# A decoder step with paged attention on one core: a second tile for the sample's new rows, key and query loads placed by rules of their own, row sums in the ring of probability tiles

## The chip, the cores and the metric

The kernel runs on 1 core of one Trainium2 chip. The metric is the time of one execution in microseconds (us) as the device measures it; three runs of the kernel before gave 3022.00, 3025.98 and 3029.27 us, median 3025.98 us. A profile is one further execution with its trace.

## The reference

One inference step of a two-layer decoder in float32: a recurrent layer (RG-LRU), then an attention layer with forgetting. It runs for a prompt (one sequence of 2048 new tokens) and for a sample (8 sequences of 8 new tokens, each behind 4096 cached tokens that lie in 32 pages of 128 rows, found through a page table). 16 heads of 64.

```python
def fox_block(q, k, v, cq, ck, q_pos, k_pos):
    s = jnp.einsum('bqhd,bkhd->bhqk', q, k).astype(jnp.float32) * (HEAD_DIM ** -0.5)
    s = s + jnp.swapaxes(cq, 1, 2)[:, :, :, None] - jnp.swapaxes(ck, 1, 2)[:, :, None, :]
    mask = k_pos[None, :] <= q_pos[:, None]
    s = jnp.where(mask[None, None], s, -jnp.inf)
    p = jax.nn.softmax(s, axis=-1)
    return jnp.einsum('bhqk,bkhd->bqhd', p.astype(v.dtype), v)
...
        past_k = cache_k[page_table].reshape(Bs, past_len, N_HEADS, HEAD_DIM)
        past_v = cache_v[page_table].reshape(Bs, past_len, N_HEADS, HEAD_DIM)
...
        y = fox_mixer(rms_norm(x, b_pre_norm[l]), k_all, v_all, cq, ck, q_pos, k_pos, b_w_in[l], b_w_out[l])
        x = x + rms_norm(y, b_post_norm[l])
```

The kernel returns the outputs of both groups, the new keys, values and log-forget rows, and the recurrent states.

## The kernel before, in words

The stages follow each other on one core: the recurrent layer in two chunks, the projections to keys, values, queries and gates, attention, the output projection. The change lies in two pieces of code that run beside each other.

**`attention` (from line 1332)** does the prompt. Work goes by units: a unit `u` is a head `h` and a quarter `qc` of 512 query rows, 64 units in all; odd heads take the quarters in the opposite order. Inside a unit each tick handles one tile of 128 keys against the 512 queries: two matmuls into a score bank `st` (lines 1592 and 1593), an exponential on ScalarE (line 1601) into a probability tile `p` (tag `p`, 6 buffers) or, for the first tick of a unit, into `acc`; after four ticks, and two more of delay, the product with the values (`ops`, line 1612), and additions of `p` to `acc` on GpSimd (POOL). A head has 40 ticks.

The exponential needs each query row's maximum first. `top` (line 1421) works it out some 18 to 26 ticks ahead of the unit: matmuls `sx` of the queries `qbt` with the keys `kbt` (line 1431), and a maximum on VectorE (lines 1433 and 1435). The `sx` banks are 3. `tops` then writes the maxima into four more rows of `qbt` (`mps`, lines 1448 and 1450). So `qbt` is needed by `top` first and by the unit's score matmuls later; it has 6 buffers (`NQ`), `kbt` has 2, one for even and one for odd heads. `load_unit` (line 1413) and `load_keys` (lines 1399 and 1400) fill them. Before the change `advance` loads the next unit's `qbt` when the first `top` of a unit is due, and the keys of the next head are loaded behind the first tick of a head. Other loads (`load_low`, `load_head`, the gates at line 1521) are emitted inside `with paged()`.

When a head's four units are through, `total` sums their `acc` over partitions (`tot`, line 1481), ScalarE copies the result to `cs` (line 1484), a tile of its own, and a DMA spreads it into `sums` (line 1490); `norm` makes reciprocals (line 1495), sends them through a DMA (line 1501) and a matmul `rp` (line 1505), and stores the gated output (line 1511).

**`decode` (from line 1039)** does the sample: 16 turns, one for each sequence and half of the heads; turns from the fourth on run beside the projections and attention (`ahead` is true there). A turn brings 32 pages of keys and 32 of values in groups of four by DMAs on the SP queue (`pages`, line 1093, 256 KB each, tile `raw`, 4 buffers of a group each), transposes the keys on VectorE (`ktr`, line 1180), multiplies (`dS`, line 1148), makes a softmax, and multiplies with the pages of values (`dO`, line 1262). The 8 new rows of keys and of values of the sample come by `new_rows` (line 1103) into `rawn`, one zeroed tile for both: the keys' rows are read by a transpose at the turn's fifth page group (line 1158), the values' rows by a product at the turn's end (line 1270).

Order: all loads of attention and decode but the very first are issued on the SP queue, one after the other; a DMA whose buffer is in use holds all behind it. A scheduler fixes the order of every queue when the program is built: it takes instructions by priority (the order in which the code emits them) and by its own estimate of when each is ready, so that one may overtake another that would have to wait. Buffers with one tag are handed out in the order in which the tiles are asked for. `paged()` adds an edge: what is issued inside stands behind the newest page that has been emitted.

Of the kernel before, what the change touches and what calls it, by code (L numbers as in the profile page):

```python
# [11 lines left out]
F32 = mybir.dt.float32  # L12
# [8 lines left out]
P = 128  # L21
# [6 lines left out]
H = 16  # L28
# [20 lines left out]
LEAD = 18  # L49
# [7 lines left out]
NP = 6  # L57
ADD = "G"
OG = 1
NQ = 6  # L60
# [21 lines left out]
def f(ap):  # L82

    return ap.bitcast(F32)
# [3 lines left out]
def tile_hawk_fox(  # L88
# [8 lines left out]
    V, A, G, T, S = nc.vector, nc.scalar, nc.gpsimd, nc.tensor, nc.sync  # L97
# [19 lines left out]
    def paged():  # L117

        return tc.issue_after(place["S"]) if "S" in place else ExitStack()
# [49 lines left out]
    def dt_(name, shape):  # L169
        return dram.tile(shape, F32, name=name, tag=name)  # L170
# [13 lines left out]
    ks_d, vs_d = dt_("ksd", [NSAMP, D]), dt_("vsd", [NSAMP, D])  # L184
# [37 lines left out]
    def sbuf(es, name, side=None):  # L222
        return es.enter_context(tc.tile_pool(name=name, bufs=1, side=side, reuse_waits="tile"))
# [819 lines left out]
    def decode(es, turns, nraw, nktr, ahead):  # L1043
        pool = sbuf(es, "dec", "right")
# [4 lines left out]
        qmask = pool.tile([P, DS], F32, name="qmask")  # L1049
        V.tensor_reduce(qmask[:, :], ident[:, :].rearrange("p (a q) -> p q a", q=DS), axis=AX.X, op=ALU.add)  # L1050

        rawn = pool.tile([P, 512], F32, name="rawn")
        G.memset(rawn[:, :], 0.0)
        pcs = [pool.tile([P, 64], F32, name=f"dpc{i}") for i in range(2)]
        for pc in pcs:
            G.memset(pc[:, :], 0.0)
# [43 lines left out]
        def new_rows(rows, b, hg):  # L1100

            assert known >= {("k" if rows is ks_d else "v", hg * 2 + c) for c in range(2)}
            S.dma_start(rawn[:DS, :], rows[b * DS:(b + 1) * DS, hg * 512:(hg + 1) * 512])
            return rawn

# [228 lines left out]
    def attention(es):  # L1334
        pool = sbuf(es, "att")
# [4 lines left out]
        pool.tile([P, 512], F32, name="acc", tag="acc", bufs=NACC)  # L1340
        pool.tile([P, 512], F32, name="p", tag="p", bufs=NP)
        pool.tile([P, 512], F32, name="oT", tag="oT", bufs=5)
        pool.tile([P, 512], F32, name="cs", tag="cs")
        pool.tile([P, 512], F32, name="sgt", tag="sgt", bufs=2)
        vvs = [pool.tile([P, 16, HD], F32, name=f"vvt{i}") for i in range(2)]
        pool.tile([P, SEQ], F32R, name="ka", tag="ka", bufs=2)
# [36 lines left out]
        units = [(h, qc) for h in range(H) for qc in ((0, 1, 2, 3) if h % 2 == 0 else (3, 2, 1, 0))]  # L1383
# [5 lines left out]
        def halves(h):  # L1389
            return ((0, half), (half, SEQ)) if h == 0 else ((0, SEQ),)  # L1390
# [4 lines left out]
        def load_keys(h):  # L1395
            kb = kbs[h % 2]
            loaded.add(h)
            for lo, hi in halves(h):
                queue[0].dma_start(f(kb[0:64, lo:hi]), kd_d[h * HD:(h + 1) * HD, 1, lo:hi])
                queue[0].dma_start(f(kb[64:67, lo:hi]), nc_d[h, :, lo:hi])  # L1400
# [9 lines left out]
        def load_unit(u):  # L1410
            h, qc = units[u]
            assert u < done[2] + NQ
            queue[0].dma_start(f(qbs[u % NQ][0:64, :]), qd_d[h * HD:(h + 1) * HD, 0, qc * 512:(qc + 1) * 512])

        def load_low(u):
            if u < len(units):
                h, qc = units[u]
                qa = qas[u] = pool.tile([P, 512], F32R, name="qa", tag="qa", bufs=4)
                queue[0].dma_start(f(qa[:, :]), qd_d[h * HD:(h + 1) * HD, :, qc * 512:(qc + 1) * 512].rearrange("d x t -> (d x) t"))
# [56 lines left out]
        def total(h2, sums, todo, single):  # L1476


            ps = ps3.tile([P, 512], F32, name="tot", tag="sx", bufs=3)
            for qc, acc in todo:  # L1480
                T.matmul(ps[qc * 32:(qc + 1) * 32, :], ones[:, :32], acc[:, :], start=True, stop=True)
            cs = pool.tile([P, 512], F32, name="cs", tag="cs")
            rows = slice(0, P) if len(todo) == 4 else slice(qc * 32, (qc + 1) * 32)
            A.copy(cs[rows, :], ps[rows, :])
            if single:
                for qc, acc in todo:
                    j = qc * 2 + h2
                    S.dma_start(sums[j * 16:(j + 1) * 16, :], cs[qc * 32:qc * 32 + 1, :].rearrange("o (r c) -> o r c", r=16))
            else:
                S.dma_start(sums[h2 * HD:(h2 + 1) * HD, :], cs[:, :].rearrange("(q z) (r c) -> z q r c", z=32, r=16)[0])  # L1490
# [37 lines left out]
        nks = [(qc + 1) * 4 for _, qc in units]  # L1528
        start = [sum(nks[:u]) for u in range(len(units))]
        done = [0, 0, 0]  # L1530

        def advance(tick):

            need = 0
            for u in range(len(units)):
                need = max(need, start[u] + nks[u] - 2 * max(0, start[u] - min(LEAD, RAMP + tick) - tick))
                if start[u] > tick + 40:
                    break
            while done[0] < min(need, len(tasks)):
                u, j, ck = tasks[done[0]]  # L1540
                while done[1] <= min(u + 1, len(units) - 1):
                    load_unit(done[1])
                    done[1] += 1
                top(u, j, ck)
                done[0] += 1

        load_keys(0)
        tick = 0
# [12 lines left out]
        def scores_bank():  # L1561

            if dec_done:
                wide[0] += 1
                if wide[0] % 2:
                    return psum["dec"].tile([P, 512], F32, name="st", tag="do"[wide[0] // 2 % 2], bufs=1)
            return ps3.tile([P, 512], F32, name="st", tag="st", bufs=2)
# [3 lines left out]
        def loads():  # L1571
            while lows[0] < len(units):
                v = lows[0]
                if tick < (start[v - 2] if v < 4 else min(max(start[v - 2], start[v - 3] + AFT), start[v] - 3)):
                    break
                with paged():
                    load_low(v)
                lows[0] += 1
            h, k = divmod(tick, 40)
            if k == 16 and h + 1 < H:  # L1580
                with paged():
                    load_head(h + 1)

        for u, (h, qc) in enumerate(units):
            for k in range(nks[u]):
                loads()
                ka, kb = heads[h], kbs[h % 2]
                qa, qb = qas[u], qbs[u % NQ]
                lo = max(0, k - qc * 4) * P
                ks = slice(k * P, (k + 1) * P)  # L1590
                ps = scores_bank()
                place["T"] = T.matmul(ps[:, lo:], ka[:, ks], qa[:, lo:], start=True, stop=False).ins  # L1592
                T.matmul(ps[:, lo:], kb[:, ks], qb[:, lo:], start=False, stop=(k < qc * 4))  # L1593
                if k >= qc * 4:
                    T.matmul(ps[:, lo:lo + P], identB[:, :], causal[:, :], start=False, stop=True)
                done[2] = u + (k == nks[u] - 1)
                if k == 0:
                    p = acc = pool.tile([P, 512], F32, name="acc", tag="acc", bufs=NACC)
                else:
                    p = pool.tile([P, 512], F32, name="p", tag="p", bufs=NP)  # L1600
                pair.append((k, lo, p, A.activation(p[:, lo:], ps[:, lo:], AF.Exp)))  # L1601

                def product(u=u, h=h, todo=pair, acc=acc, last=(k == nks[u] - 1)):


                    nonlocal ops
                    if todo[0][0] == 0:
                        ops = ops2[:, u % 2 * 256:u % 2 * 256 + 256]

                    def mm(k, lo, p, r):  # L1610
                        a0 = (lo // P + 1 - r) // 2
                        return T.matmul(ops[r * HD:(r + 1) * HD, a0 * P:], vvs[h % 2][:, k, :],  # L1612
                                        p[:, :].rearrange("p (a r c) -> p a r c", a=2, r=2)[:, a0:, r, :],
                                        start=(k == 0), stop=(last and k == todo[-1][0] - 1 + r))

                    together([partial(mm, k, lo, p, r) for k, lo, p, _ in todo for r in range(2) if lo <= (2 + r) * P],
                             [todo[-1][3]])
                    for k, lo, p, _ in todo:
                        if k:
                            tt(a_l(), acc[:, lo:], acc[:, lo:], p[:, lo:], ALU.add)  # L1620
                    if last:
                        finish(u, ops, acc)

                if k % 4 == 3:
                    later.after(2, product)
                    pair = []
                before = done[0]
                advance(tick)
                tick += 1
                later.tick()  # L1630
                if k + sum(nks[u - u % 4:u]) == 0 and h + 1 < H:
                    load_keys(h + 1)
                yield 4.1 * (512 - lo) * 0.42 + (done[0] - before) * 213

    lent, dec_done = {}, []
# [1 line left out]
    rows = [(NSAMP, None, x1s_d[:, :], ys_flat)]  # L1637
# [151 lines left out]
    done = 9  # L1789
# [6 lines left out]
    done = max(done, 41)  # L1796
# [104 lines left out]
```

## Time and profile before

| | us |
|---|---|
| median of 3 runs | 3025.98 |
| profiled execution, its own time | 3028.43 |
| span of that execution's trace | 3026.4 |
| TensorE busy (PE) | 2803.4 |
| VectorE busy (DVE) | 1805.5 |
| ScalarE busy (ACT) | 1269.9 |
| GpSimd busy (POOL) | 1084.4 |

The span is the trace from its first to its last instruction; the execution's own time is 2.0 us longer. PE is TensorE's matmuls, PEld its weight loads, SPq the SP queue as it issues DMAs. An arrow in a row (`out<-in`) names what is written and read, `x16` counts instructions, and the bracket behind a row of the timeline gives the idle time of the engine before it with what ended it. A row of waits gives who waited, for whom, the total, the number and the longest. The granted clock is TensorE's, as a share of full speed.

### The profile page before, as it was taken

How to read it: one execution, taken by the hardware profiler on the slowest of the kernel's cores; microseconds unless marked ns; L12 is line 12 of the kernel's file. 1: busy time of each engine (PE TensorE's matmuls, PEld its weight loads, DVE VectorE, ACT ScalarE, POOL GpSimd, SP SyncE). 2: the span in 40 equal slices, each digit the busy share in tenths (PEclk: the TensorE clock that was granted, in tenths of full speed). 3: DMA queues.
4: the chain of work that ended last, by engine and by line, in shares of the span. 5: the costliest groups of instructions: out<-in, count | busy, mean ns of one | idle time of the engine just before them, and what ended most of it. 6: DMA issues, size and time to landing. Idle time of an engine off the chain costs nothing.

```text
span 3026.4 us, 60467 instructions
## 1 busy us (share of the span) xinstructions
PE 2803.4 (93%) x21614; PEld 2252.1 (74%) x21614; DVE 1805.5 (60%) x4012; ACT 1269.9 (42%) x2874; POOL 1084.4 (36%) x1199
## 2 busy tenths in 40 slices
PE   6998999998997999999999699998998999999998
PEld 5997789988887997888889556665665666565687
DVE  6877455425427775676564466656776756655344
ACT  4665342222125665534333234444544444355321
POOL 1653201000002653100000245665575656659422
PEclk9999999999998999999999889999999999999999
DMA  4224546888863226699999968898899888874343
GB/s 123 79 88 133 171 126 191 256 263 281 278 216 91 89 88 194 209 313 338 332 346 326 279 209 243 248 282 255 250 291 287 267 251 265 260 247 122 98 145 110
DMA packets 479103, 653.79 MB, mean 216 GB/s; under 512 B 91291, under 2 KB 277020, under 8 KB 471525
## 3 DMA queue, kind: packets, MB, share of 16 engines
q1 hardware_dynamic: 475174, 644.26, 67.4%
q10 hardware_dynamic: 3340, 3.56, 0.4%
q8 instruction: 171, 2.80, 0.4%
q0 software_dynamic: 288, 2.10, 0.2%
q14 instruction: 130, 1.06, 0.1%
HBM read 514.22 MB, written 135.16 MB: 215 GB/s over the span
## 4 chain that ended last, share of the span: by engine, by line
PE 59%; DMA 16%; DVE 9%; ACT 6%; SPq 5%; issue 3%; POOL 1%; ACTq 0%; DVEq 0%; POOLq 0%
PE ops L1612 7%; PE st L1592 4%; PE y L383 4%; PE y L384 4%; PE y L385 4%; DMA raw<-in_cache_k_dram 4%; PE sx L1431 4%; PE dO L1262 3%; DMA raw<-in_cache_v_dram 3%; PE st L1593 3%; PE dS L1148 3%; PE kv L383 3%; PE kv L385 3%; PE kv L384 3%; SPq L1093 2%
## 5 line engine op out<-in xcount | busy, mean ns | idle before, releaser
L108 POOL TENSOR_TENSOR acc<-acc,p 128x512 f32<-128x512 f32 (+3 forms) x576 | 640.9, 1114 | 347.7 <-PE ops L1612 211.2
L1601 ACT ACTIVATE p<-st 128x512 f32<-128x512 f32 (+3 forms) x576 | 291.3, 525 | 400.1 <-PE st L1593 177.5
L1180 DVE STREAM_TRANSPOSE ktr<-raw 128x1024 f32<-128x1024 f32 x256 | 308.2, 1226 | 125.1 <-DMA raw<-in_cache_k_dram 116.5
L1433 DVE TENSOR_REDUCE mxs<-sx 128x1 f32<-128x512 f32 x384 | 255.0, 681 | 141.0 <-PE sx L1431 139.6
L383 PE MATMUL kv<-wh,xh 128*128 128x256 f32 (+3 forms) x1088 | 310.0, 288 | 6.4 <-ACT wh L427 4.7
L384 PE MATMUL kv<-wl,xh 128*128 128x256 f32 (+3 forms) x1088 | 309.3, 287 | 5.7 <-DVE wl L428 5.7
L385 PE MATMUL kv<-wh,xl 128*128 128x256 f32 (+3 forms) x1088 | 309.6, 286 | 2.7 <-DMA xl<-xld 2.7
L1592 PE MATMUL st<-qa,ka 128*128 128x512 f32 (+3 forms) x640 | 269.9, 422 | 13.3 <-ACT p L1601 7.5
L1612 PE MATMUL ops<-p,vvt 128*64 128x256 f32 (+1 forms) x2176 | 262.9, 369 | 1.0 <-ACT p L1601 0.7
L1431 PE MATMUL sx<-kbt,qbt 96*128 96x512 f32 (+3 forms) x640 | 229.2, 416 | 29.9 <-DMA qbt<-qd 24.2
L1113 POOL TENSOR_TENSOR qw<-qb,amask 128x128 f32<-128x128 f32 x64 | 29.1, 460 | 618.1 <-PE dS L1148 325.3
L428 DVE SCALAR_TENSOR_TENSOR wl<-wst,gv,wh 128x256 fp32r<-128x256 f32 (+1 forms) x384 | 169.4, 504 | 131.8 <-ACT wh L427 131.5
L427 ACT ACTIVATE wh<-wst,gv 128x256 fp32r<-128x256 f32 (+1 forms) x384 | 164.6, 499 | 190.2 <-DMA wst<-in_w_kv_dram 72.7
L1593 PE MATMUL st<-qbt,kbt 128*128 128x512 f32 (+3 forms) x640 | 236.9, 370 | 0.0
L383 PE MATMUL qg<-xh,wh 128*128 128x512 f32 (+2 forms) x640 | 229.4, 359 | 0.0
L384 PE MATMUL qg<-xl,wh 128*128 128x512 f32 (+2 forms) x640 | 228.2, 357 | 0.0
L385 PE MATMUL qg<-xh,wl 128*128 128x512 f32 (+2 forms) x640 | 227.5, 356 | 0.6 <-DVE wl L428 0.6
L1612 PEld LDWEIGHTS ops<-p,vvt 128*64 128x64 f32 x2176 | 161.5, 141 | 88.2 <-issue 19.8
L383 PEld LDWEIGHTS kv<-wh,xh 128*128 128x128 f32 (+1 forms) x1088 | 203.5, 188 | 13.2 <-ACT wh L427 6.8
L384 PEld LDWEIGHTS kv<-wl,xh 128*128 128x128 f32 (+1 forms) x1088 | 203.2, 188 | 10.1 <-DVE wl L428 6.9
L385 PEld LDWEIGHTS kv<-wh,xl 128*128 128x128 f32 (+1 forms) x1088 | 204.8, 188 | 7.0 <-issue 3.7
L1592 PEld LDWEIGHTS st<-qa,ka 128*128 128x128 f32 x640 | 123.7, 193 | 112.8 <-issue 54.4
(297 smaller groups left out, 6356.3 us busy)
## 6 DMA issues: line engine op xcount, KB each, us to landing
raw<-in_cache_k_dram SPq DMA_DIRECT2D x512, 256.0 KB
raw<-in_cache_v_dram SPq DMA_DIRECT2D x512, 256.0 KB
wst<-in_w_kv_dram SPq DMA_DIRECT2D x48, 512.0 KB
wst<-in_b_w_in_dram SPq DMA_DIRECT2D x48, 512.0 KB
xt<-in_x_prompt_dram SPq DMA_DIRECT2D x32, 512.0 KB
wst<-in_a_w_in_dram SPq DMA_DIRECT2D x64, 256.0 KB
out_dram<-kf SPq DMA_DIRECT2D x128, 128.0 KB
sc<-cd SPq DMA_DIRECT2D x16, 1024.0 KB
```

The source lines that it names most:

```text
L108: eng.tensor_tensor(out, a, b, op=op)
L383: T.matmul(ps, lh(k), rh(k), start=(k == 0), stop=False)
L384: T.matmul(ps, lh(k), rl(k), start=False, stop=False)
L385: T.matmul(ps, ll(k), rh(k), start=False, stop=(k == nk - 1))
L428: V.scalar_tensor_tensor(wl[:, k, :], st[:, k, :], gk, f(wh[:, k, :]), op0=ALU.mult, op1=ALU.subtract)
L1180: behind("V", V.transpose(t.kts[pp][:, n], raw[:, :, pp * 256:(pp + 1) * 256]).ins)
L1431: T.matmul(ps[:, :w], qb[0:96, j * P:(j + 1) * P], kb[0:96, ck * 512:ck * 512 + w], start=True, stop=True)
L1433: place["V"] = V.reduce_max(mx[:, j, ck:ck + 1], ps[:, :w], axis=AX.X).ins
L1592: place["T"] = T.matmul(ps[:, lo:], ka[:, ks], qa[:, lo:], start=True, stop=False).ins
L1593: T.matmul(ps[:, lo:], kb[:, ks], qb[:, lo:], start=False, stop=(k < qc * 4))
L1601: pair.append((k, lo, p, A.activation(p[:, lo:], ps[:, lo:], AF.Exp)))
L1612: return T.matmul(ops[r * HD:(r + 1) * HD, a0 * P:], vvs[h % 2][:, k, :], p[:, :].rearrange("p (a r c) -> p a r c", a=2, r=2)[:, a0:, r, : ...
```

## The change

Four edits:

- In the second `decode` (`ahead`) `rawn` becomes two tiles; the keys' rows go to the last, the values' rows to the first.
- The tile `cs` loses its own buffer and is taken from tag `p`, the ring of six probability tiles.
- `advance` now loads a unit's queries only where they are still missing; the regular place is in `loads`, at the head of a tick: as soon as the unit's start is no more than `LEAD` + half its ticks + 7 ticks away and a buffer is handed back, inside `paged()`.
- The next head's keys are loaded in `loads` at tick 6 of a head, inside `paged()`, and no longer behind its first tick.

```diff
-        rawn = pool.tile([P, 512], F32, name="rawn")
-        G.memset(rawn[:, :], 0.0)
+        rawns = [pool.tile([P, 512], F32, name=f"rawn{i}") for i in range(2 if ahead else 1)]
+        for rawn in rawns:
+            G.memset(rawn[:, :], 0.0)
...
+            rawn = rawns[-1 if rows is ks_d else 0]
             S.dma_start(rawn[:DS, :], rows[b * DS:(b + 1) * DS, hg * 512:(hg + 1) * 512])
...
-        pool.tile([P, 512], F32, name="cs", tag="cs")
...
-            cs = pool.tile([P, 512], F32, name="cs", tag="cs")
+            cs = pool.tile([P, 512], F32, name="cs", tag="p", bufs=NP)
...
-                while done[1] <= min(u + 1, len(units) - 1):
+                while done[1] <= u:
                     load_unit(done[1])
...
+            while done[1] < len(units) and done[1] < done[2] + NQ and tick >= start[done[1]] - LEAD - nks[done[1]] // 2 - 7:
+                with paged():
+                    load_unit(done[1])
+                done[1] += 1
             h, k = divmod(tick, 40)
+            if k == 6 and h + 1 < H:
+                with paged():
+                    load_keys(h + 1)
...
-                if k + sum(nks[u - u % 4:u]) == 0 and h + 1 < H:
-                    load_keys(h + 1)
```

The lines of the changed kernel lie one to eight higher than those of the kernel before. Three places show what the change does to the order.

The SP queue early in attention, between a group of key pages and the next group of value pages (`raw`). Before, with the two query tiles, and the values' rows in the one `rawn`:

```order
L1413 DMA qbt0_19863<-qd_78 64x512
L1103 DMA rawn_14345<-vsd_83 8x512
L1413 DMA qbt1_19864<-qd_78 64x512
L1086 TENSOR_LOAD pt1_115
L1093 ISA
L1093 DMA raw_20436<-in_cache_v_dram 128x512
```

Now:

```order
L1105 DMA rawn0_14345<-vsd_83 8x512
L1105 DMA rawn1_14346<-ksd_82 8x512
L1087 TENSOR_LOAD pt1_115
L1094 ISA
L1094 DMA raw_20437<-in_cache_v_dram 128x512
```

Both row DMAs stand there one behind the other (before, the keys' rows stood two pages further ahead, among the key pages), and the two query loads have moved behind later pages.

ScalarE's queue at the end of the third head, with the copy `cs` and the exponentials around it. Before (the exponentials into `p_22848` and its followers run ahead of the copy):

```order
L1601 ACTIVATE p_22766<-st_22763 128x512
L1601 ACTIVATE p_22843<-st_22840 128x512
L1601 ACTIVATE p_22848<-st_22845 128x512
L1601 ACTIVATE p_22865<-st_22862 128x512
L1601 ACTIVATE p_22870<-st_22867 128x512
L1601 ACTIVATE p_22891<-st_22888 128x512
L1601 ACTIVATE p_22904<-st_22901 128x512
L1601 ACTIVATE p_23002<-st_22999 128x512
L1601 ACTIVATE p_23014<-st_23011 128x512
L1601 ACTIVATE p_23026<-st_23023 128x512
L1601 ACTIVATE p_23052<-st_23048 128x512
L1450 ACTIVATE qbt1_19864<-mps_22728,less_19908 4x128 x4
```

and behind these stands the copy `cs_22773`. Now (`p_22842` here is what `p_22843` was):

```order
L1609 ACTIVATE p_22760<-st_22757 128x512
L1609 ACTIVATE p_22765<-st_22762 128x512
L1451 ACTIVATE qbt1_19865<-mps_22729,less_19909 4x128 x4
L1485 COPY cs_22772<-tot_22767 128x512
L1609 ACTIVATE p_22842<-st_22839 128x512
L1609 ACTIVATE p_22847<-st_22844 128x512
L1609 ACTIVATE p_22864<-st_22861 128x512
L1609 ACTIVATE p_22871<-st_22868 128x512
```

The copy has moved ahead of ten exponentials. The last row is the one that takes the copy's buffer again, so it waits for the DMA that reads `cs`.

TensorE's queue at the end of the first head, around the sums `tot`. Before:

```order
L1448 MATMUL mps<-ident,mrow_19901 128x128
L1481 MATMUL tot<-acc,ones 32x512 x4
L1431 MATMUL sx<-kbt_19870,qbt_19863 128x512
L1612 MATMUL ops<-p,vvt_19860 64x256 x8
L1592 MATMUL st<-qa,ka 128x512
L1593 MATMUL st<-qbt_19867,kbt_19870 128x512
```

Now:

```order
L1449 MATMUL mps<-ident,mrow_19902 128x128
L1482 MATMUL tot<-acc,ones 32x512 x4
L1432 MATMUL sx<-kbt_19871,qbt_19864 128x512
L1432 MATMUL sx<-kbt_19871,qbt_19864 128x128
L1432 MATMUL sx<-kbt_19871,qbt_19864 128x512
L1432 MATMUL sx<-kbt_19871,qbt_19864 128x256
L1432 MATMUL sx<-kbt_19871,qbt_19864 128x512
L1432 MATMUL sx<-kbt_19871,qbt_19864 128x384
L1432 MATMUL sx<-kbt_19871,qbt_19864 128x512
L1620 MATMUL ops<-acc,vvt_19861 64x256 x2
L1620 MATMUL ops<-p,vvt_19861 64x256 x6
L1600 MATMUL st<-qa,ka 128x512
```

Seven row-maximum products stand between `tot` and the next score product, where one stood; the `sx` of the unit after have been pulled forward.

## The prediction

> **What bounds the kernel now.** I read the page's busy times first, then the windows of the stage that the change touches, then who waits for whom there, then the order in time around the waits. Columns of a window: engine busy us and instructions, then the granted TensorE clock, DMA share and GB/s.
>
> ```profile
> PE 2803.4 (93%) x21614; PEld 2252.1 (74%) x21614; DVE 1805.5 (60%) x4012; ACT 1269.9 (42%) x2874; POOL 1084.4 (36%) x1199
> 1800.00:2700.00 900.00, 846.08 (x7720) 540.37 (x7720) 587.35 (x1252) 409.88 (x1017) 561.91 (x535) 0.97 0.85 264
> PE dO L1262 <- DMA raw<-in_cache_v_dram: 19.1, 12, 3.1
> PE st L1592 <- ACT p L1601: 5.6, 16, 0.8
> ```
>
> TensorE is the bound: 2803 of 3026 us over the whole program, and 846 of 900 us in the stage where attention runs beside the sample's decode. There it stands still for 54 us. The largest single cause is 19.1 us in 12 waits of the value products (dO) for pages of cached values. Such a page is late when the SP queue, which issues all pages, stood behind something else:
>
> ```profile
> SPq L1093 <- PE dO L1262: 33.0, 12, 7.3
> SPq L1413 <- PE st L1595: 20.7, 9, 5.3
> SPq L1399 <- PE sx L1431: 16.5, 2, 16.0
> SPq L1413 <- PE sx L1431: 13.7, 13, 6.1
> SPq L1103 <- DVE mrow L1444: 9.0, 1, 9.0
> ```
>
> Between 1740 and 2740 us the queue stood behind query loads (L1413), key loads (L1399) and the sample's new rows (L1103) for some 60 us (the last four rows), and behind page buffers that a product had not yet freed (the first row) for 33. The change touches the three former and not the latter. A wait of SP costs nothing by itself; it costs where a product then stands still.
>
> **The change part by part.** First, the tile of new rows. Early in attention the queue had this order (start, duration, line, operation):
>
> ```profile
> 1760.57 0.45 SPq L1413 DMA_DIRECT2D qbt<-qd  x1
> 1770.05 0.30 SPq L1103 DMA_DIRECT2D rawn<-vsd  x1
> 1771.67 0.45 SPq L1413 DMA_DIRECT2D qbt<-qd  x1
> 1780.41 2.34 SPq L1093 DMA_DIRECT2D raw<-in_cache_v_dram  x4
> 1800.79 1.07 PE L1262 MATMUL dO<-raw,sx 128*32 128x256 f32 x16 [2.18 <-DMA raw<-in_cache_v_dram]
> 1798.00:1808.00 10.00, 7.82 (x47) 4.83 (x46) 5.92 (x11) 2.88 (x5) 1.36 (x2) 0.83 1.03 346
> ```
>
> Three small DMAs took 20 us of the queue: the values' rows had to wait until the keys' rows had been read from the one tile, and both query tiles until their last readers were through. In the changed order both row DMAs stand directly ahead of those value pages, each with a tile of its own, and the two query loads stand behind later pages. I take back the 2.18 us wait, and the clock that followed it: 0.83 granted over 10 us is 1.7 us of lost work. Together **3.9 us**. The same pattern with a query load alone:
>
> ```profile
> 1910.90 6.26 SPq L1413 DMA_DIRECT2D qbt<-qd  x1
> 1917.76 1.94 SPq L1093 DMA_DIRECT2D raw<-in_cache_v_dram  x4
> 1924.24 1.20 PE L1262 MATMUL dO<-raw,sx 128*32 128x256 f32 x16 [2.08 <-DMA raw<-in_cache_v_dram]
> 1924.00:1932.00 8.00, 7.76 (x140) 5.71 (x144) 2.13 (x6) 2.79 (x7) 5.03 (x7) 0.79 1.02 319
> ```
>
> The load held the queue for 6.26 us, the pages went out behind it, and TensorE waited 2.08 us; 0.79 over 8 us is 1.7 us more. I take all of it, **3.8 us**. Two other places I take in part:
>
> ```profile
> 1980.10 1.09 SPq L1413 DMA_DIRECT2D qbt<-qd  x1
> 1988.37 1.94 PE L1262 MATMUL dO<-raw,sx 128*32 128x256 f32 x16 [3.10 <-DMA raw<-in_cache_v_dram]
> 1986.00:1996.00 10.00, 7.63 (x94) 5.27 (x94) 2.90 (x7) 1.13 (x3) 1.74 (x2) 0.66 0.83 258
> 2097.71 1.07 PE L1262 MATMUL dO<-raw,sx 128*32 128x256 f32 x16 [0.91 <-DMA raw<-in_cache_v_dram]
> 2106.64 1.07 PE L1262 MATMUL dO<-raw,sx 128*32 128x256 f32 x16 [1.86 <-DMA raw<-in_cache_v_dram]
> 2117.49 1.07 PE L1262 MATMUL dO<-raw,sx 128*32 128x256 f32 x16 [0.76 <-DMA raw<-in_cache_v_dram]
> 2126.07 1.07 PE L1262 MATMUL dO<-raw,sx 128*32 128x256 f32 x16 [1.15 <-DMA raw<-in_cache_v_dram]
> 2090.00:2130.00 40.00, 35.11 (x390) 22.12 (x388) 22.45 (x40) 13.42 (x29) 29.12 (x25) 1.00 0.85 273
> ```
>
> At 1988 the query load held the queue for only 1.09 us: I take 1.1 of the 3.1 us, and half of the clock (0.66 over 10 us is 3.4), **2.8 us**. The four waits around 2110 sum to 4.7 us at full clock; a row DMA, a key load and a query load lie among their pages, and I take half, **2.3 us**. The other dO waits, 19.1 − 12.0 = 7.1 us, I leave. Gain: 3.9 + 3.8 + 2.8 + 2.3 = **12.8 us**.
>
> What is late next is what the change adds. The copy of the row sums (cs) now takes a place in the ring of six probability tiles, and holds it until its DMA has landed:
>
> ```profile
> 1909.52 0.58 ACT L1484 COPY cs<-tot 128x512 f32<-128x512 f32 x1
> 1920.28 0.69 SPq L1490 DMA_DIRECT2D sums<-cs  x1
> 1925.18 0.35 DVE L1495 RECIPROCAL sums<-sums 128x32 f32<-128x32 f32 x1 [2.60 <-DMA sums<-cs]
> 2187.69 0.58 ACT L1484 COPY cs<-tot 128x512 f32<-128x512 f32 x1
> 2188.30 0.62 SPq L1490 DMA_DIRECT2D sums<-cs  x1
> ```
>
> From copy to issue it took between 0.0 us (2188) and 10.2 us (1920), and another 4.2 us to land (1920.97 to 1925.18). In the changed order the place is wanted again by the fourth score tile behind the copy at six of the first thirteen head ends, later at the others. Queued behind the waiting exponential on ScalarE are the next ones, and TensorE stands once its two score banks are full. Those two banks and the row-maximum products beside them are the cover; without it this costs up to 5 us a head, 0 to 30 us at the six. I take 1.8 us, by the rows nearest to it: the exponentials' present waits for their ring cost TensorE 5.6 us in 16 places.
>
> Further, the exponentials behind a copy may no longer pass it, and the order fills the gap with row-maximum products (sx): over the whole order, places with six or more of them between two score products go from 2 to 12.
>
> ```profile
> L1433 DVE TENSOR_REDUCE mxs<-sx 128x1 f32<-128x512 f32 x313 | 208.1, 681 | 118.0 <-PE sx L1431 116.9
> L1431 PE MATMUL sx<-kbt,qbt 96*128 96x512 f32 (+3 forms) x527 | 185.5, 409 | 5.3 <-DVE mxs L1435 2.6 <-DVE mxs L1433 1.3 <-ACT qbt L1450 0.8
> ```
>
> VectorE takes 0.68 us each, TensorE 0.41, with three banks between: six in a row cost at most 3 × 0.27 = 0.8 us, ten places 0 to 8 us. I take 1.2, since all present waits of that kind are 2.6 + 1.3 us. Queries and keys loaded later I cost at nothing (0 to 17 us, see the rivals); the cover is SP's lead over TensorE, which the 33.0 us row shows, since there SP waits for TensorE. ScalarE issues one query load less at the start of attention; that is at most one issue (0.45 us above), taken at nothing. The second clearing of a tile is one POOL instruction on an engine 36% busy. Cost: **3.0 us**.
>
> Sum against the profiled execution's own time: 3028.4 − 12.8 + 3.0 = 3018.6. That execution was 2.4 us above the median of the runs, so I give **3016 us** beside 3026.
>
> Of the 12.8 us, 5.1 are clock. The Trainium skill, page "TensorE: Matmul & The Clock Gate", section "Part 1: The HAM clock gate (the "warmup" mystery)", says that the rate halves after about one idle window of 3.4 us. By that rule none of these waits would cost clock, and the result would be 3021. The trace does not agree: behind waits of 2.18 and 2.08 us the windows show 0.83 and 0.79; behind four shorter ones 1.00. I go by the windows.
>
> **The rivals.** *The page buffers take over (no change).* A query load that no longer blocks only lets the queue reach the next page, whose buffer may be in use: the 33.0 us row. And this row pair shows 16 us of blocked queue behind a key load, after which the only wait of TensorE in the next 37 us was the third row:
>
> ```profile
> 2637.12 0.39 SPq L1419 DMA_DIRECT2D qa<-qd  x1
> 2653.51 0.46 SPq L1399 DMA_DIRECT2D kbt<-kd  x1
> PE st L1592 <- ACT p L1601: 0.6, 1, 0.6
> ```
>
> Also the key loads hardly move in the order: 0 to 6 pages later. If gain and cost are both about 3 us: **3026**. Chance 0.14. With the clock kept as the page's rule has it (3021), 0.04 more.
>
> *The sums hold the ring (slower).* There are as many score tiles as sx products, 527 in 900 us, one per 1.7 us; the fourth tile wants the place 6.9 us after the copy. A DMA out 9 us after it, as it nearly was at 1920, has landed at 9 + 0.7 + 4.2 = 13.9, so the exponentials stop for 7.0 us; two banks cover 3.4, leaving 3.6 us and 1.7 us of clock. At four of the six heads that is 21 us: 3028.4 − 12.8 + 1.2 + 21 − 2.4 = **3035**. It decides once the DMA leaves more than some 5 us after the copy. For it: the order puts the copies 3 to 10 score tiles earlier, their DMAs only 0 to 8 pages. Against: at 2188 the queue was there at once. Chance 0.20.
>
> *Queries come too late (slower).* The load for unit 15 stood behind page 536 of the 1024 and now stands behind page 568, its first use behind the 131st score tile; unit 56's load went from page 980 to 1004, its use is behind the 535th. At the present pace these are:
>
> ```profile
> 1975.31 0.50 PE L1592 MATMUL st<-qa,ka 128*128 128x512 f32 x1 [0.28 <-ACT p L1601]
> 2675.77 0.33 SPq L1093 DMA_DIRECT2D raw<-in_cache_v_dram  x1
> 2678.01 0.23 PE L1592 MATMUL st<-qa,ka 128*128 128x128 f32 x1
> ```
>
> Page 568 is out at 1980.1, 4.8 us after the first; page 1004 only 2.2 us ahead of the last. With 4.5 us to land (1919.7 to 1924.2) that is 9.3 and 2.3 us, with 3.4 and 1.7 us of clock 16.7 us, so 3028.4 − 9.8 + 16.7 − 2.4 = **3033**. It decides once SP is less than 4.5 us ahead. Chance 0.17.
>
> **How the numbers follow.** Forecast 0.45, no change 0.18, ring 0.20, queries 0.17. Low end: the remaining 7.1 us of dO waits and their clock (3.4) go too and the costs are nil, 3016 − 13.5 = 3002. High end: the slower rivals with some of each other, 3044. Faster by over 0.2% 0.45, within 0.2% (6 us, about what a measurement of this kernel can tell from no change) 0.18, slower 0.37.
>
> **What would show it.** Right: the queue's waits under the query loads and row DMAs fall from 43 us (three rows above) to under 20, dO waits for value pages to about 9 us, and the windows around 1800 and 1924 show a full clock. Ring: TensorE waits for exponentials rise well above 5.6 us, and SP's sums follow the copies by 8 us. Queries: a wait of sx for a query DMA appears inside the stage, where none is now. Wrong altogether: dO still waits some 19 us.

## The result, and the profile after

| | before | after |
|---|---|---|
| median us (lowest to highest) | 3024.66 (3022.00 to 3029.27) | 3102.89 (3095.99 to 3111.29) |
| profiled execution: own time, span, clock | 3028.43, 3026.4, 0.969 | 3095.99, 3094.3, 0.960 |

The ratio is 1.0258, 95% interval 1.0225 to 1.0291: slower by 78 us, where 3016 was forecast and the range ended at 3044. The loss lies between the first and the last of the 640 score products (`st`). There TensorE's trace reads:

| first to last score product | length | TensorE busy | idle | longer than before, behind head ends | elsewhere |
|---|---|---|---|---|---|
| before | 1074.8 | 1011.7 | 63.0 | | |
| after | 1146.1 | 1040.4 | 105.7 | 84.3 | -12.9 |

"Behind head ends" are the first 20 score products of each of the heads 1 to 15, nearly half of the work. All of the loss is there. The 84.3 us hold some work that the order has moved there from elsewhere (4096 matmuls of TensorE where there were 3966), which is why the rest is shorter than before; net it is 71 us, 4.8 us a head. In the whole stretch 43 us of the loss are idle time, and 29 us are the same work (8863 and 8866 matmuls) at a lower clock.

Views of the kernel after, first the windows of the same stretches as before (busy us and instructions of PE, PEld, DVE, ACT, POOL, then the granted clock, DMA share, GB/s):

```profile
1800.00:2700.00 900.00, 819.60 (x7384) 522.47 (x7386) 566.49 (x1192) 386.13 (x954) 531.02 (x509) 0.95 0.81 249
1798.00:1808.00 10.00, 9.44 (x56) 5.48 (x56) 7.30 (x14) 4.62 (x11) 2.18 (x2) 0.97 0.77 271
1924.00:1932.00 8.00, 8.00 (x122) 4.58 (x120) 2.52 (x8) 4.13 (x10) 5.28 (x7) 1.00 0.85 267
```

The two places where I had counted the gain run at 0.97 and 1.00 of the clock, and yet TensorE does 336 matmuls fewer in the 900 us. Who waits for whom there, TensorE first:

```profile
PE mps L1449 <- DVE mrow L1445: 21.0, 8, 7.6
PE st L1600 <- ACT p L1609: 12.2, 20, 2.6
PE sx L1432 <- DVE mxs L1436: 11.8, 8, 4.5
...
PE dO L1264 <- DMA raw<-in_cache_v_dram: 5.8, 2, 3.1
```

The waits for value pages (dO) fell from 19.1 to 5.8 us, by more than the forecast. In their place TensorE waits for the row maxima from VectorE. The row for `mps` was this before, with those of two other engines:

```profile
PE mps L1448 <- DVE mrow L1444: 5.2, 3, 3.4
```

```profile
DVE ktr L1180 <- DMA raw<-in_cache_k_dram: 7.1, 4, 4.0
```

```profile
ACT acc L1601 <- PE tot L1481: 4.4, 6, 1.3
```

After, VectorE's key transposes wait for pages, and ScalarE for the sums (`tot`):

```profile
DVE ktr L1182 <- DMA raw<-in_cache_k_dram: 41.1, 13, 6.6
```

```profile
ACT acc L1609 <- PE tot L1482: 20.8, 5, 8.1
ACT p L1609 <- DMA sums<-cs: 11.7, 5, 4.0
```

The longest of TensorE's waits shows how they hang together. TensorE at a head's end (start, duration, instruction; the bracket is the idle time before it):

```profile
2556.15 0.79 PE L1432 MATMUL sx<-kbt,qbt 96*128 96x512 f32 x3
2556.78 0.39 PE L1600 MATMUL st<-qa,ka 128*128 128x512 f32 x1
2557.01 0.39 PE L1601 MATMUL st<-qbt,kbt 128*128 128x512 f32 x1
2557.24 0.39 PE L1600 MATMUL st<-qa,ka 128*128 128x512 f32 x1
2557.47 0.40 PE L1601 MATMUL st<-qbt,kbt 128*128 128x512 f32 x1
2557.70 1.25 PE L1432 MATMUL sx<-kbt,qbt 96*128 96x512 f32 x3
2566.51 0.47 PE L1449 MATMUL mps<-ident,mrow 128*128 128x128 f32 x1 [7.57 <-DVE mrow L1445]
2566.91 1.94 PE L1482 MATMUL tot<-acc,ones 128*32 128x512 f32 x8
2568.78 1.65 PE L1432 MATMUL sx<-kbt,qbt 96*128 96x512 f32 x3
```

VectorE meanwhile:

```profile
2558.26 1.28 DVE L1434 TENSOR_REDUCE mxs<-sx 128x1 f32<-128x512 f32 x2
2559.45 2.36 DVE L1182 STREAM_TRANSPOSE ktr<-raw 128x1024 f32<-128x1024 f32 x2
2564.37 1.25 DVE L1182 STREAM_TRANSPOSE ktr<-raw 128x1024 f32<-128x1024 f32 x1 [2.55 <-issue]
2565.54 0.67 DVE L1436 CUSTOM_DVE_ANT_0 sx<-sx,maskb 128x512 f32<-128x512 f32 x1
2566.12 0.13 DVE L1436 DVE_READ_ACCUMULATOR2_ANT mxs<- 128x1 f32 x1
2566.29 0.17 DVE L1445 TENSOR_REDUCE mrow<-mxs 128x4 f32<-128x12 f32 x1
```

And ScalarE:

```profile
2567.02 1.11 ACT L1451 ACTIVATE qbt<-mps,less 4x128 fp32r<-4x128 f32 x4 [9.94 <-PE mps L1449]
2568.99 0.59 ACT L1485 COPY cs<-tot 128x512 f32<-128x512 f32 x1 [0.86 <-PE tot L1482]
2569.48 1.09 ACT L1609 ACTIVATE p<-st 128x512 f32<-128x512 f32 x2
```

Both score banks were full at 2557.9. Their exponentials stand in ScalarE's queue behind four writes of maxima (L1451), which wait for `mps`, and behind the copy `cs`, which waits for `tot`. On TensorE `tot` stands behind `mps`, and `mps` waits for the last of a bunch of row maxima, which on VectorE stands behind three key transposes. Before the third of them VectorE itself stood idle for 2.55 us, for which the row names no cause ("issue"). TensorE has nothing else between. And it does not run at full speed when it goes on:

```profile
2545.00:2558.00 13.00, 12.95 (x105) 8.58 (x96) 10.47 (x18) 5.53 (x12) 11.03 (x10) 1.00 0.99 339
2567.00:2571.00 4.00, 4.00 (x15) 1.36 (x17) 1.39 (x4) 2.68 (x7) 0.00 (x0) 0.50 1.00 279
2571.00:2574.00 3.00, 3.00 (x17) 1.53 (x14) 1.31 (x2) 0.00 (x0) 2.00 (x2) 0.60 1.05 329
2574.00:2578.00 4.00, 4.00 (x85) 2.50 (x84) 0.00 (x0) 1.20 (x2) 3.77 (x4) 1.00 0.88 206
```

### The profile page after: what moved, and what is told of

Its sections match the earlier page's. It is cut to its first block, busy times and chain, and to the rows that moved or that the text cites. A ratio compares the mean times of both kernels' runs of the same rounds, so it can differ in the third digit from the quotient of the medians.

```text
span 3094.3 us, 60439 instructions
## 1 busy us (share of the span) xinstructions
PE 2824.8 (91%) x21614; PEld 2257.3 (73%) x21614; DVE 1800.5 (58%) x4012; ACT 1268.9 (41%) x2874; POOL 1083.0 (35%) x1200
## 4 chain that ended last, share of the span: by engine, by line
PE 44%; DMA 20%; DVE 8%; SPq 5%; issue 3%; ACT 3%; POOL 2%; DVEq 0%; ACTq 0%; POOLq 0%
PE ops L1620 6%; DMA raw<-in_cache_k_dram 5%; PE st L1600 4%; PE sx L1432 3%; PE y L384 3%; PE y L383 3%; PE y L385 3%; PE dO L1264 3%; DMA raw<-in_cache_v_dram 3%; PE st L1601 3%; PE dS L1150 3%; SPq L1094 2%; DVE ktr L1182 2%; PE qg L383 2%; PE qg L384 2%
## 5 line engine op out<-in xcount | busy, mean ns | idle before, releaser
L1620 PE MATMUL ops<-p,vvt 128*64 128x256 f32 (+1 forms) x2176 | 273.7, 379 | 1.6 <-ACT p L1609 1.5
L1620 PEld LDWEIGHTS ops<-p,vvt 128*64 128x64 f32 x2176 | 167.8, 146 | 93.5 <-issue 29.0
```

## The experiments

My theory (A): the place of `cs` in the ring makes the loss, by the order that it forces. Rivals: the loads (B), and the ring's lack of places (C). The kernel before was measured again beside each group of runs (medians 3024.59 to 3030.34 us). The differences below are the ratio to it, with its 95% interval, times 3026 us.

**Which edit.** e1 has the ring alone:

```diff
-        pool.tile([P, 512], F32, name="cs", tag="cs")
...
-            cs = pool.tile([P, 512], F32, name="cs", tag="cs")
+            cs = pool.tile([P, 512], F32, name="cs", tag="p", bufs=NP)
```

> The kernel before with one edit alone: the copy cs takes a place in the ring of probability tiles (tag p) instead of its own tile. Theory A (this edit makes the loss: in the order, probability tiles that are asked for behind cs may not pass it, and row maxima and the sample's key products are pulled up to 10 score tiles ahead at the head ends): 3085 to 3110 us, with VectorE's waits of ktr for key pages well above the 7 us of before and SP waiting for the copy. Theory B (the loss comes from the later and paged loads of queries and keys): 3020 to 3035 us, near the kernel before.

Measured: 3105.77 us, +77 (71 to 83). e2 has the query and key loads of the change's diff alone:

```diff
+            while done[1] < len(units) and done[1] < done[2] + NQ and tick >= start[done[1]] - LEAD - nks[done[1]] // 2 - 7:
+                with paged():
+                    load_unit(done[1])
...
+            if k == 6 and h + 1 < H:
+                with paged():
+                    load_keys(h + 1)
```

> The kernel before with the new rules for query and key loads alone; cs keeps its own tile, one rawn. Theory A (cs in the ring is the cause): 3012 to 3027 us, and no bunches of row maxima, since the order of TensorE hardly moves. Theory B (late loads are the cause): 3085 to 3110 us, with sx waiting for query DMAs in the stage.

Measured: 3048.68 us, +21 (16 to 25), between the two theories. So the ring alone makes the whole loss, but the loads are no gain either. (Together, in the change, the two do not add up: 78.)

**Places or order.** e3 is e1 with a seventh place:

```diff
-NP = 6
+NP = 7
```

> As e1 (cs in the ring of probability tiles, nothing else changed), but the ring has seven places instead of six, so that as many are left to the probability tiles as before. The order of TensorE is nearly the same as in e1. Theory A (the order in which the ring's places are handed out, not their number, does the harm): as slow as e1, within 10 us, 3080 to 3110 us. Theory C (one place too few: the exponentials wait until the DMA of the sums has freed it): back to 3020 to 3035 us.

Measured: 3099.50 us, +70 (62 to 77). The waits of exponentials for the DMA of the sums, 11.7 us in the kernel after, were already small in e1 (first row), which is as slow; in e3 (the other rows) they are all but gone:

```profile
ACT p L1600 <- DMA sums<-cs: 2.5, 1, 2.5
...
ACT acc L1600 <- PE tot L1480: 24.5, 6, 6.9
ACT cs L1483 <- PE tot L1480: 0.9, 1, 0.9
ACT p L1600 <- DMA sums<-cs: 0.7, 1, 0.7
```

So theory C falls. e4 has all edits but the ring (the diff is against the kernel after):

```diff
-            cs = pool.tile([P, 512], F32, name="cs", tag="p", bufs=NP)
+            cs = todo[-1][1]
```

> All edits of the change except the ring: two tiles for the new rows, the new loads of queries and keys; the copy cs is written into the last acc tile of the head, which the sums have just read, so it needs neither a tile of its own nor a place in the ring. Theory A: the gain of my prediction without the loss, 3008 to 3022 us, dO waits for value pages below 10 us. Theory B (loads): 3085 to 3110 us. If the two rawn tiles and the loads only gain where cs has no part, but page buffers take over: 3022 to 3030 us.

Measured: 3045.91 us, +21 (16 to 25): without the ring only what e2 costs is left, and the forecast gain is not there.

**The order itself.** e10 is e1 with the copy, its request for a place and its DMA six score tiles later (at all but the last two heads); `norm`, which needs the sums, comes six later too:

```diff
+            def copied():
                 cs = pool.tile([P, 512], F32, name="cs", tag="p", bufs=NP)
...
...
+            copied() if single else later.after(6, copied)
```

> As e1 (cs in the ring of six probability tiles), but of all head ends but the last two the copy and its place in the ring are asked for six score tiles later than the matmuls of the sums. In the order there is then one bunch of six or more row maxima where e1 has eight (two in the kernel before), and the sample's key products stand on average 0.8 score tiles earlier than before, where e1 has 1.8. Theory A (the harm is the order that the ring's place forces: score products and exponentials asked for behind cs stand behind it, the rest is pulled ahead): a good part of e1's 78 us goes, 3040 to 3070 us. Theory C (a copy that shares the ring with the probability tiles, whatever the order): 3090 to 3110 us.

Measured: 3041.90 us, +18 (11 to 25). The same ring of six, the same copy, and three quarters of the loss are gone; in its trace 1.9 us are lost behind head ends and 21.2 elsewhere. e11 moves the copy of e1 to VectorE:

```diff
-            A.copy(cs[rows, :], ps[rows, :])
+            V.tensor_copy(cs[rows, :], ps[rows, :])
```

> As e1, but VectorE makes the copy cs instead of ScalarE, so no exponential stands behind the copy in ScalarE's queue; the order of TensorE is pulled apart as in e1 (key products on average 1.9 score tiles earlier). Theory A2 (TensorE's own order does the harm: row maxima, sums and key products in one piece, with no score product between them): as slow as e1, 3085 to 3115 us. Theory A4 (the harm is the convoy on ScalarE: exponentials that stand behind a copy that waits for the sums): 3030 to 3060 us.

Measured: 3107.52 us, +79 (67 to 90). So the exponentials that stand behind a copy in ScalarE's queue are not the cause. e11 leaves others standing, those behind the writes of maxima, which wait for `mps`:

```profile
ACT qbt L1449 <- PE mps L1447: 54.9, 19, 10.9
```

In the kernel before this row was 39.0 us with 3.7 us as the longest. They are long where `mps` is late. (The copy also costs a little on VectorE: `sx` waits 3.3 us for it in e11.) With the ring's places (e3) and the copy (e11) out, and three quarters of the loss gone when the place is asked for later (e10), the order of TensorE and VectorE is what is left; that is an inference, for no run changes TensorE's order alone.

**Pages or bunches.** e8 and e9 let the key transposes of the second decode read a constant:

```diff
-                    behind("V", V.transpose(t.kts[pp][:, n], raw[:, :, pp * 256:(pp + 1) * 256]).ins)
+                    if ahead:
+                        kt_ = t.kts[pp][:, n].rearrange("p a (b c) -> p (a b) c", c=P)
+                        behind("V", V.transpose(kt_, ident[:, :].unsqueeze(1).to_broadcast([P, 8, P])).ins)
+                    else:
+                        behind("V", V.transpose(t.kts[pp][:, n], raw[:, :, pp * 256:(pp + 1) * 256]).ins)
```

> The kernel before, but the key transposes (ktr) of the second decode read a constant matrix instead of the key pages, which are loaded all the same; the products with the cached keys are therefore not the reference's. VectorE then never waits for a key page, and a key page's buffer is free when it has landed. It is the base for e9. Theory A: 2990 to 3025 us, somewhat faster than the kernel before, since key pages cost little there (7 us of VectorE's waits).

> As e8, with the one edit of e1 (cs in the ring of probability tiles). In the order, the key products and the sums stand as much earlier against e8 as those of e1 stand against the kernel before (up to 10 score tiles at the head ends). Theory A1 (the harm is that row maxima stand in VectorE's queue behind transposes that wait for key pages, of which the bunched order wants more than the queue has brought): at most 25 us slower than e8. Theory A2 (the harm is the bunching of products on TensorE and VectorE itself, whatever the pages do): 60 to 85 us slower than e8, as e1 against the kernel before (78).

Measured: e8 3041.91 us, +16 (11 to 21); e9 3100.07 us, +73 (66 to 80). e9 is 58 us above e8, where A1 had at most 25 and A2 60 to 85, and 61 of the 63 us between their two traces lie behind head ends. No wait of a transpose for a key page is left in either; TensorE's first rows in e9 are:

```profile
PE mps L1451 <- DVE mrow L1447: 19.8, 8, 5.1
PE sx L1434 <- DVE mxs L1436: 15.7, 11, 6.2
```

So A1, which I had read out of the 41.1 us row, fails: the loss without any wait for key pages is 58 us. By the difference of the two pairs (77 and 58) the late key pages make some 20 us, an estimate with about 10 us either way. My expectation of e8 was wrong too: it is 16 us slower. In its trace these lie ahead of the stage: its first score product starts at 1761.9 us, before at 1749.2, and from the first to the last its trace takes 1075.7 us, before 1074.8. What costs there was not pursued.

**The gain that did not come.** e5 has the second tile for new rows alone, with `cs` as in e4:

```diff
+        rawns = [pool.tile([P, 512], F32, name=f"rawn{i}") for i in range(2 if ahead else 1)]
...
+            cs = todo[-1][1]
```

> The kernel before with the second tile for the new rows alone (the copy cs is written into the last acc of the head, as in e4, which leaves TensorE's order as before and makes the room). Theory D (in e2 and e4 the moved loads are what costs; the second rawn is harmless): the gain of my first term, 3.9 us, or less: 3020 to 3029 us. Theory E (where cs is written into acc, something else is lost, and that is the 18 us of e4): 3038 to 3050 us.

Measured: 3031.34 us beside 3030.34, +1 (-4 to 6). No gain shows, though the interval just reaches the 3.9 us of my first term. e12 gives the query tiles a seventh:

```diff
-NQ = 6
+NQ = 7
...
+            cs = todo[-1][1]
```

> The kernel before with a seventh query tile (qbt) in the room of cs, whose copy goes into the last acc of the head. The orders of TensorE and VectorE stay as before; the query loads go out up to 28 pages earlier, since their buffer is free earlier, so SP no longer stands under them. Theory F (my gain: the queue's waits under query loads make pages late): SP's waits under the query loads fall from 49.5 us to under 15, dO waits from 19 to about 10, time 3015 to 3024 us. Theory G (the queue then waits for page buffers instead, and nothing is gained): 3024 to 3033 us, with more of SP's waits on its page line (148.7 us in the kernel before).

Measured: 3025.46 us, 0 (-6 to 6), but SP's waits under query loads only fell from 49.5 to 44.5 us, so it does not tell F from G. e2 does: there they fell to 18.9, and the next rows show what took their place:

```profile
SPq L1093 <- PE dO L1262: 43.6, 11, 9.9
SPq L1093 <- PE sx L1431: 21.8, 11, 7.3
```

```profile
PE dO L1262 <- DMA raw<-in_cache_v_dram: 18.4, 7, 4.3
```

All waits on SP's page line rose from 148.7 to 181.6 us and those on the row line from 29.7 to 42.9, and dO waits 18.4 us, as before. That is what G says of the queue; the time of e2 cannot speak for it, since e2 loses 21 us by other means.

**What the loads cost.** e6 and e7 have the query loads and the key loads of e2 alone (the first and the second piece of its diff).

> The kernel before with the new rule for query loads alone; the keys of the next head are loaded where they were. Theory D1 (queries): most of e2's 19 us, 3040 to 3050 us, with the loss between the 360th and the 560th score tile as in e2. Theory D2 (keys): 3018 to 3030 us.

> The kernel before with the new place of the key loads alone (tick 6 of a head, behind the newest page). Theory D1 (queries are e2's loss): no difference, 3022 to 3031 us, since the order of TensorE is the same and the key loads move by 0 to 4 pages. Theory D2 (keys): 3038 to 3050 us.

Measured: e6 3035.53 us, +8 (2 to 14); e7 3034.88 us, +5 (0 to 9); both lie outside the ranges of both theories. e13 takes `with paged():` off the query loads of e2, e14 adds it alone to the query loads of the kernel before:

```diff
-                with paged():
-                    load_unit(done[1])
+                load_unit(done[1])
```

```diff
-                    load_unit(done[1])
+                    with paged():
+                        load_unit(done[1])
```

> As e2 (the new rules for query and key loads alone), but the query loads are not held behind the newest page: the order then places them up to 28 pages earlier than before instead of 16 to 32 pages later at every second head, and the order of TensorE is that of the kernel before at all heads but the last. Theory D3 (e2's 20 us come from queries that are held back, by the order that this forces at the middle heads or by their lateness): back to 3020 to 3032 us. Theory D4 (they come from the key loads, or from the rest of the new rules): 3038 to 3052 us.

> The kernel before with one thing added: its query loads, at their old place in the code, are held behind the newest page. They then stand up to 40 pages later than before (e2: up to 32), the order has seven places with six or more row maxima between two score products (before 2, e2 3, e1 8), and the key products stand 0.3 score tiles earlier on average. Theory D3 (held queries cost, by the bunches they make): slower than e2, 3045 to 3075 us. Theory D4: 3022 to 3034 us.

Measured: e13 3034.06 us, +7 (2 to 12), 2 us above the range of D3 and about as much as the key loads of e7, which it has too; e14 3061.65 us, +37 (30 to 44). So holding the query loads back costs. No wait of `sx` for a query DMA shows up in e14 inside the stage; its order has bunches again, and TensorE waits for row maxima longer than before (5.2, 2.6 and 1.3 us):

```profile
PE mps L1448 <- DVE mrow L1444: 9.0, 3, 4.8
PE sx L1431 <- DVE mxs L1435: 8.5, 7, 4.1
...
PE sx L1431 <- DVE mxs L1433: 5.6, 9, 0.9
```

## Why the prediction was wrong

- **The bound** held: TensorE sets the end, by its waits and its clock.
- **The gain, 12.8 us**, was read from true rows, but failed at the step from SP's wait to TensorE's. I took it that a query load or row DMA that no longer blocks lets the value pages come earlier. The runs show that the queue then stands at the next page's buffer or row (e2), as the rival of the page buffers said, and no gain of the second row tile (e5). e8 shows the step from the other side. There the waits of dO for value pages are gone, and still the stage is no shorter (1075.7 us against 1074.8), because other waits of TensorE have grown (the first row was 5.6 us before, the second 1.3):

```profile
PE st L1596 <- ACT p L1605: 9.9, 29, 0.7
PE sx L1435 <- DVE mxs L1437: 9.7, 11, 2.3
...
PE dO L1266 <- DMA raw<-in_cache_v_dram: 0.2, 1, 0.2
```

  That dO waits fell to 5.8 us, one of my signs of being right, is no evidence for the step either: in e1, with neither of those edits, they are

```profile
PE dO L1262 <- DMA raw<-in_cache_v_dram: 10.0, 2, 5.2
```

  and 16.6 us in e3. A TensorE that is late itself waits less for pages, so in a slower kernel this sign cannot tell.
- **The ring, 1.8 us**, and the rival that grew from it (3035) had the right edit and the wrong mechanism: I priced how long the copy holds its place. That wait is 11.7 us of ScalarE's in the kernel after and 2.5 us in e1, which is as slow, and six or seven places give about the same time (e3); so it is not what costs.
- **The bunches, 1.2 us**: this is the term that failed. The order had shown them (places with six or more `sx` go from 2 to 12), and I priced them by throughput, 3 × 0.27 us each. The runs give 58 (without waits for key pages) to 78 us for the order that the ring forces, these bunches included. As the trace at 2557.70 reads, a bunch is not paid by the 0.27 us that VectorE is slower, but by the time until VectorE delivers its last maximum, with nothing left for TensorE: the score products, which had been the cover for every `sx`, were what the order had taken out, and `mps` and `tot` stood inside. That was 7.57 us of idle time there, and then seven us at 0.50 to 0.60 of the clock. The number of bunches alone does not set the price: the planned orders of e1 and e14 had eight and seven, and they cost 77 and 37 us.
- **Later loads, nothing**: +21 us alone. The rival "queries come too late" had the edit right and the way wrong: in the kernel after there is one wait of `sx` for a query of 2.0 us. e14 and e13 point to the order that a held load forces.
- **The clock**: I took 5.1 us back at places where the clock was indeed 0.97 to 1.00 afterwards, and paid 29 us elsewhere. Against it I had set a rule of the Trainium skill, page "TensorE: Matmul & The Clock Gate", section "Part 1: The HAM clock gate (the "warmup" mystery)": half rate after about one idle window of 3.4 us. The 7.57 us gap agrees with that rule. The gap at 2301.80 does not; it was 2.58 us long and was followed by

```profile
2304.40:2308.00 3.60, 3.60 (x10) 2.26 (x12) 2.50 (x8) 2.04 (x6) 0.00 (x0) 0.50 0.98 322
```

What stays open: how the 21 us of e2 divide beyond e6, e7 and e13; the 18 us that e10 still loses away from the head ends (its exponentials keep TensorE waiting for 18.0 us instead of 5.6); why the 21 us of the loads do not add to the ring's 77; and what in the order sets the price besides the number of bunches. None of the kernels is faster than the one before; e5 and e12 equal it, and e7 cannot be told from it.

## What to carry to other kernels

A tile that is moved into another ring takes part in that ring's order of requests, not only in its number of places: look at what stands between two products of the main stream before and after, and price a bunch by the time until its last result, not by the difference of two throughputs. Where one queue feeds several streams, a wait taken from one load can come back at the next one, as it did here (e2): look whether that one's buffer is free. A fall of one wait in the slower kernel proves nothing about the edit; the edit alone does.

## What was not expected of the hardware

After idle gaps of TensorE of 2.58 and 7.57 us the granted clock was 0.50 to 0.60 for some 4 to 7 us (the windows above). The length of the gap alone does not decide: after one of 3.09 us in the same trace the clock stayed at 1.00:

```profile
2663.85 1.07 PE L1264 MATMUL dO<-raw,sx 128*32 128x256 f32 x16 [3.09 <-DMA raw<-in_cache_v_dram]
2663.80:2668.00 4.20, 4.15 (x33) 2.77 (x35) 2.36 (x5) 1.59 (x3) 3.00 (x3) 1.00 0.91 318
```

Over all score products the gaps cost some two thirds more than their own length: 43 us of added idle time came with 29 us of added busy time for the same matmuls.
